# In a product-key expert layer, blocks of u are transposed in place, six buffers take gathered half rows, and their products stand four points behind the gathers

## The chip, the cores and the metric

One core of one Trainium2 chip. The metric is the time of one execution in device microseconds, the median of three runs: 3521.41 us (3520.7 to 3525.29). A difference of 0.2%, about 7 us, is what a measurement of this kernel can tell from none.

## The reference

One decoder layer over 512 tokens of width 2048, in float32. The first half is a modulated RMSNorm, one projection, a short causal convolution beside differential attention, and an output projection. The second half, in which the change lies, is a product-key expert layer: each token takes 16 of 16384 single-neuron experts in each of 8 heads.

```
h2 = RMSNorm(x) * (1 + scale2) + shift2
idx, g = top 16 of the 128 x 128 key sums, softmax of their scores     # per token and head
a = <u[idx], h2>                                                       # 128 dot products of width 2048 per token
w = gelu(a) * g
x = x + gate2 * sum(w * v[idx])                                        # u, v: 16384 x 2048 each
```

## The kernel before

**Two ways for the experts.** The first TG = 160 tokens are *gathered*: for each of 128 choices the rows of u and of v that the tokens chose are fetched by an indirect DMA and used on VectorE. The other TD = 352 tokens are *dense*: all 16384 experts are computed for them on TensorE, and a table of gates (`g_dram`) zeroes those not chosen. The gathered work fills VectorE, POOL and the DMA engines beside the dense matmuls.

**The dense path** goes over 128 blocks of 128 experts, in chunks of CH = 8. A block of u (1 MB) comes by eight DMAs of 128 KB (`u_load`, L511, on SP's queue) into a tile `ur`, of which there are two (UR_BUFS). Its layout needs the 32 x 32 blocks transposed: `u_turn` transposes one half at a time (L780, VectorE) into a tile `utf`, of which there are two; `split` then writes a float32r high part (L88, ScalarE) and the rest (L89, VectorE) into `ut`, of which there are two (UT_BUFS). TensorE takes 48 matmuls per block from it (L792), ScalarE the gelu (L809), `w_block` multiplies by the gates (L824) and splits into W. After eight blocks `v_group` loads v (`vr`, L935, 512 KB, three buffers), splits it into `vs` (L88, L89) and does as many matmuls again (L945); sums go to `acc` (L961). The first NPRE = 12 blocks are transposed earlier, beside the output projection (`u_ahead`, L516: `uar` into `uat`), and kept in `u_dram`.

**The gathered path.** There are 643 steps: for 128 choices of 128 tokens, and then for 32 rounds in which the last 32 tokens are folded four times into the partitions, each choice has two half rows of u, later two of v (`gathered`, L844, [128 x 1024], issued by POOL). A half row of u is multiplied by h2 and summed (L853), one of v is multiplied by its weight and added to `gacc` (L867, L869). All use tile `gt`, of which there are GBUF = 4. A gather also waits for the last matmul of a list `pace`, so that it doesn't run ahead of TensorE; a point is added to the list four times per block in u, and once per two blocks in `v_group`, and at each point `gather_to` emits the steps that are due, the product right behind its gather.

**What sets the order.** Each engine runs its queue in order. The order in the queues is set when the kernel is built, by a scheduler that takes the instructions' priorities from the program; a row of a queue waits for semaphores. SP's queue has the loads of u, v and the gates; its DMAs take eight semaphores in turn, so that each waits for the one eight before it to have landed.

**The end.** In the last chunk `add_gathered` brings the gathered tokens' sums (a_dram for the first 128, `gacc` for the folded 32) into the result `xs`, and `store` writes it out.

## Time and profile before

| | |
|---|---|
| median of the runs | 3521.41 us |
| the profiled execution | 3524.61 us, its span 3522.6 us |
| busy: TensorE / VectorE / ScalarE / POOL | 92% / 81% / 35% / 40% |
| mean granted TensorE clock | 0.967 |
| DMA | 896.34 MB, mean 254 GB/s |
| chain that ended last | DMA 42%, VectorE 28%, TensorE 15% |

The stretch from about 1500 to 3440 us is the main loop over the blocks; the weights of the first half come before it, the end of the last chunk after it. A line is that of the kernel before; `L89` and `L88` are the helper `split`, so that its uses are told apart by their tiles. VectorE's busy share is high but below that of TensorE, and what matters is what each idle stretch waited for.

### The profile page before, as it was taken

What the parts mean: (1) busy time and instruction counts of PE and PEld (TensorE: products, weight loads), DVE (VectorE), ACT (ScalarE), POOL (GpSimd) and SP (SyncE); (2) the same over time, 40 slices, a digit from 0 to 9 for tenths busy, and PEclk for the clock granted to TensorE, in tenths of its full rate; (3) what the DMA queues carried; (4) which work ended last, traced back from release to release, by engine and by line L of the source; (5) the groups of instructions that cost most, each with busy time, mean ns of one, the idle gap of its engine ahead of it and who ended that gap; (6) DMA issues with size and microseconds to landing.
All of it is one profiled execution on the core that took longest, in us unless ns stands there. A gap on an engine that the chain in (4) does not pass through costs nothing.

```text
span 3522.6 us, 49092 instructions
## 1 busy us (share of the span) xinstructions
...
## 2 busy tenths in 40 slices
...
GB/s 288 286 229 143 254 190 178 183 177 290 252 88 68 61 122 202 264 298 323 305 315 295 310 310 299 300 287 300 306 314 313 298 307 306 326 310 319 299 302 163
DMA packets 425712, 896.34 MB, mean 254 GB/s; under 512 B 40402, under 2 KB 119167, under 8 KB 420735
## 3 DMA queue, kind: packets, MB, share of 16 engines
...
HBM read 843.47 MB, written 49.55 MB: 254 GB/s over the span
## 4 chain that ended last, share of the span: by engine, by line
DMA 42%; DVE 28%; PE 15%; issue 9%; POOL 3%; SPq 2%; ACT 1%; DVEq 0%; POOLq 0%; ACTq 0%
DMA ur<-in_expert_u_dram 14%; DMA vr<-in_expert_v_dram 9%; DMA gt<-in_expert_u_dram,idxu 6%; PE pm L457 4%; DMA ada_w<-in_w_ada_dram 4%; DMA gt<-in_expert_v_dram,idxu 4%; DVE gacc L869 3%; DVE utf L780 3%; DVE vs L89 2%; DVE gt L907 2%; DVE gt L853 2%; DVE ut L89 2%; DVE ada_acc L196 2%; PE pm L547 2%; DVE run L196 2%
## 5 line engine op out<-in xcount | busy, mean ns | idle before, releaser
L792 PE MATMUL pa<-hd,ut 128*128 128x352 f32 x6144 | 1077.3, 328 | 63.9 <-DVE ut L89 41.0
L945 PE MATMUL pv<-W,vs 128*128 128x352 f32 x6144 | 1071.4, 328 | 50.6 <-DVE vs L89 27.0
L792 PEld LDWEIGHTS pa<-hd,ut 128*128 128x128 f32 x6144 | 1015.2, 191 | 75.8 <-DVE ut L89 48.4
L945 PEld LDWEIGHTS pv<-W,vs 128*128 128x128 f32 x6144 | 1014.5, 191 | 61.2 <-DVE vs L89 32.7
L89 POOL TENSOR_TENSOR wsp<-wraw,wsp 128x1024 fp32r<-128x1024 f32 x160 | 391.5, 2449 | 562.1 <-ACT wsp L88 530.3
L844 POOL DMA_INDIRECT gt<-in_expert_u_dram,idxu x256 | 343.9, 1344 | 626.4 <-DVE gt L853 309.8
L88 ACT ACTIVATE vs<-vr 128x1024 fp32r<-128x1024 f32 x256 | 271.3, 1060 | 819.2 <-DMA vr<-in_expert_v_dram 365.8
L844 POOL DMA_INDIRECT gt<-in_expert_v_dram,idxu x256 | 340.0, 1328 | 477.9 <-DVE gacc L869 341.5
L853 DVE SCALAR_TENSOR_TENSOR gt<-gt,h2n 128x1024 f32<-128x1024 f32 x320 | 386.2, 1215 | 104.9 <-DMA gt<-in_expert_u_dram,idxu 84.8
L869 DVE SCALAR_TENSOR_TENSOR gacc<-gt,ga_a,gacc 128x1024 f32<-128x1024 f32 x316 | 400.4, 1275 | 73.9 <-DMA gt<-in_expert_v_dram,idxu 48.5
L89 DVE TENSOR_TENSOR vs<-vr,vs 128x1024 fp32r<-128x1024 f32 x256 | 309.8, 1210 | 46.9 <-ACT vs L88 46.7
L88 ACT ACTIVATE ut<-utf 128x1024 fp32r<-128x1024 f32 x232 | 244.0, 1056 | 282.3 <-DVE utf L780 169.6
L780 DVE STREAM_TRANSPOSE utf<-ur 128x1024 f32<-128x1024 f32 x232 | 286.9, 1237 | 18.2 <-DMA ur<-in_expert_u_dram 14.1
L88 ACT ACTIVATE wsp<-wraw 128x1024 fp32r<-128x1024 f32 x160 | 169.1, 1058 | 368.1 <-issue 94.7
L89 DVE TENSOR_TENSOR ut<-utf,ut 128x1024 fp32r<-128x1024 f32 x232 | 281.9, 1215 | 9.6 <-ACT ut L88 9.5
L457 PE MATMUL pm<-big,wsp 128*128 128x512 f32 x1152 | 287.6, 402 | 0.0
L457 PEld LDWEIGHTS pm<-big,wsp 128*128 128x128 f32 x1152 | 215.2, 192 | 42.6 <-issue 0.2
L196 DVE SCALAR_TENSOR_TENSOR ada_acc<-ada_w,scol,ada_acc 128x512 f32<-128x512 f32 x195 | 208.3, 1068 | 28.5 <-DMA ada_w<-in_w_ada_dram 25.1
L245 PE MATMUL pqk<-wsp,big 128*128 128x512 f32 x768 | 193.3, 411 | 21.3 <-DVE qk L291 12.9
L701 PE MATMUL pm<-big,wsp 128*128 128x512 f32 x768 | 188.2, 402 | 16.1 <-POOL wsp L89 14.5
L245 PEld LDWEIGHTS pqk<-wsp,big 128*128 128x128 f32 x768 | 150.6, 199 | 57.6 <-DVE qk L291 15.9
L701 PEld LDWEIGHTS pm<-big,wsp 128*128 128x128 f32 x768 | 146.2, 193 | 48.5 <-POOL wsp L89 17.0
(274 smaller groups left out, 3195.4 us busy)
## 6 DMA issues: line engine op xcount, KB each, us to landing
vr<-in_expert_v_dram SPq DMA_DIRECT2D x256, 512.0 KB, 10.0
ur<-in_expert_u_dram SPq DMA_DIRECT2D x928, 128.0 KB, 9.2
...
g<-g_dram SPq DMA_DIRECT2D x32, 704.0 KB, 13.6
...
```

The costliest lines, as they stand in the source:

```text
L88: hi = nc.scalar.activation(dst[:, 0], src, AF.Copy)
L89: (eng or nc.vector).tensor_tensor(out=dst[:, 1], in0=src, in1=dst[:, 0].bitcast(F32), op=OP.subtract)
L196: nc.vector.scalar_tensor_tensor(new, wt[:, k], s, old, op0=OP.mult, op1=OP.add)
L245: nc.tensor.matmul(banks[i], hT[kk][:, a, i * P:(i + 1) * P], ws[:, b, k], start=(kk == last[0] and n == 0), stop=(kk == last[1] and n == 2))
L457: nc.tensor.matmul(banks[n2], ws[:, a, k, n2 * P:(n2 + 1) * P], hT[kk][:, b], start=(kk == 0 and n == 0), stop=(kk == KC - 1 and n == 2))
L701: nc.tensor.matmul(banks[j], ws[:, a, k, j * P:(j + 1) * P], h2T[kk][:, b], start=(kk == 0 and n == 0), stop=(kk == KC - 1 and n == 2))
L780: nc.vector.transpose(t, UR[0][:, :, q * 256:(q + 1) * 256].rearrange("p b (c r) -> p c b r", r=32))
L792: mm = nc.tensor.matmul(pa[:, :TD], ut[:, a, j], hd[k][:, b], start=(k == 0 and n == 0), stop=(k == KC - 1 and n == 2))
L844: d = nc.gpsimd.indirect_dma_start(out=t, out_offset=None, in_=src, in_offset=bass.IndirectOffsetOnAxis(ap=gidx[g][:, j:j + 1], axis=0), e ...
L853: nc.vector.scalar_tensor_tensor(t, t, 1.0, h2n[:, f * D // 2:(f + 1) * D // 2], op0=OP.mult, op1=OP.mult, accum_out=ga_a[:, f, j:j + 1])
L869: nc.vector.scalar_tensor_tensor(gacc[:, s], t, a, gacc[:, s], op0=OP.mult, op1=OP.add)
L945: mm = nc.tensor.matmul(pv[j // 2][:, j % 2, :TD], vs[:, a, bb, j * P:(j + 1) * P], W[e0 // 2][:, m, bb], start=(b == 0 and n == 0), stop= ...
```

## The change

- `u_turn` no longer has a tile `utf`: half a block is transposed in place inside `ur` (contiguous runs of 256), and `split` reads `ur` in the order that `utf` had. So `ur` is free for the next load only when both halves are split; before, when both were transposed.
- `u_ahead` transposes in place too; `uat` is gone, `uar` has three buffers; `u_dram` holds the other layout.
- The room of `utf` goes to two more `gt`: GBUF is 6.
- `gather_u` and `gather_v` give back the product as a function. `gather_to` holds it back until the list `pace` is LAG = 4 points longer, or six are held, or a step needs them all; it is then placed after the last point's matmul in the scheduler's order (no semaphore).
- The a_dram loads of `add_gathered` use the tiles `ot` of `store` (four of them).

```diff
-GBUF = 4
+GBUF = 6
+LAG = 4
-PU_BUFS = 1
+PU_BUFS = 3
-UTF_BUFS = 2
...
         def u_ahead(e):
-            ur = pu.tile([P, 4, 512], F32, name="uar")
+            ur = pu.tile([P, 4, 512], F32, name="uar", bufs=PU_BUFS)
             u_load(ur, e)
-            t = pu.tile([P, 4, 4, 4, 32], F32, name="uat", bufs=PU_BUFS)
-            for q in range(4):
-                u_quarter(t[:, q], ur, q)
-            nc.sync.dma_start(u_dram[e], t.rearrange("p q c b r -> p (q c b r)"))
+            for b in range(4):
+                nc.vector.transpose(ur[:, b], ur[:, b])
+            nc.sync.dma_start(u_dram[e], ur.rearrange("p b d -> p (b d)"))
...
-            if e < NPRE:
-                t = UR[0][:, 2 * q:2 * q + 2].rearrange("p a (c b r) -> p (a c) b r", c=4, b=4)
-            else:
-                t = up.tile([P, 8, 4, 32], F32, name="utf", bufs=UTF_BUFS)
-                nc.vector.transpose(t, UR[0][:, :, q * 256:(q + 1) * 256].rearrange("p b (c r) -> p c b r", r=32))
-            UT[n] = up.tile([P, 2, 8, P], F32R, name="ut", bufs=UT_BUFS)
-            split(UT[n], t.rearrange("p c b r -> p c (b r)"))
+            t = UR[0][:, :, q * 256:(q + 1) * 256]
+            if e >= NPRE:
+                nc.vector.transpose(t, t)
+            UT[n] = up.tile([P, 2, 8, 4, 32], F32R, name="ut", bufs=UT_BUFS)
+            split(UT[n], t.rearrange("p b (c r) -> p c b r", r=32))
...
         def gather_u(g, j, f):
             t = gathered(expert_u, g, j, f)
-            nc.vector.scalar_tensor_tensor(t, t, 1.0, h2n[:, f * D // 2:(f + 1) * D // 2], op0=OP.mult, op1=OP.mult,
-                                           accum_out=ga_a[:, f, j:j + 1])
+            return lambda: nc.vector.scalar_tensor_tensor(t, t, 1.0, h2n[:, f * D // 2:(f + 1) * D // 2],
+                                                          op0=OP.mult, op1=OP.mult, accum_out=ga_a[:, f, j:j + 1])
...
         done = [0]
+        held_back = []
+
+        def use_next():
+            i = held_back.pop(0)[1]()
+            if pace:
+                tc.add_manual_dep(i.ins, pace[-1].ins.name, ORDER, reason="rows have landed")
 
         def gather_to(blocks):
             first = 0.55 * CH
             frac = min(1.0, max(0.0, (blocks - first) / (NK - first - CH)))
+            while held_back and held_back[0][0] + LAG <= len(pace):
+                use_next()
             while done[0] < math.ceil(len(steps) * frac):
                 f, a = steps[done[0]]
-                f(*a)
+                while held_back and (len(held_back) == GBUF or f in (gather_w, gather_next)):
+                    use_next()
+                use = f(*a)
+                if use is not None:
+                    held_back.append((len(pace), use))
                 done[0] += 1
+            while held_back and frac == 1.0:
+                use_next()
...
-                ar = fin.tile([P, 512], F32, name="ar")
+                ar = fin.tile([P, T], F32, name="ot", bufs=4)
```

**VectorE's queue, a piece of the main loop.** Before: the first row transposes the second half of one block of u and so frees its `ur`; the second transposition begins the next block, the third ends it. `gacc<-gt` are products of gathered rows (they wait for a DMASW semaphore, the gather's landing, and for VectorE itself).

```order
L780 STREAM_TRANSPOSE utf<-ur 128x1024 [waits DVE_49]
L869 SCALAR_TENSOR_TENSOR gacc<-gt,ga_a,gacc 128x1024 [waits DMASW5_49,DVE_49]
L780 STREAM_TRANSPOSE utf<-ur 128x1024 [waits DMAHW4_49,DMAHW3_49,DMAHW5_49,DMAHW2_49,DMAHW6_49,DMAHW1_49,DMAHW7_49,DMAHW0_49,DVE_49]
L869 SCALAR_TENSOR_TENSOR gacc<-gt,ga_a,gacc 128x1024 [waits DMASW6_49,DVE_49]
L89 TENSOR_TENSOR ut<-utf,ut 128x1024 [waits PE_49,Activation_49]
L869 SCALAR_TENSOR_TENSOR gacc<-gt,ga_a,gacc 128x1024 [waits DMASW7_49,DVE_49]
L961 TENSOR_TENSOR acc<-acc,pv 128x704 [waits PE_49]
L869 SCALAR_TENSOR_TENSOR gacc<-gt,ga_a,gacc 128x1024 [waits DMASW0_49,DVE_49]
L961 TENSOR_TENSOR acc<-acc,pv 128x704 [waits PE_49]
L780 STREAM_TRANSPOSE utf<-ur 128x1024 [waits DVE_49]
```

Of the change, the same queue: the first row splits the second half of a block and frees its `ur`; the last is the first transposition of the block that is loaded into that very tile.

```order
L89 TENSOR_TENSOR ut<-ur,ut 128x1024 [waits PE_49,Activation_49]
L862 SCALAR_TENSOR_TENSOR gacc<-gt,ga_a,gacc 128x1024 [waits DMASW0_49,DVE_49]
L862 SCALAR_TENSOR_TENSOR gacc<-gt,ga_a,gacc 128x1024 [waits DMASW1_49,DVE_49]
L89 TENSOR_TENSOR vs<-vr,vs 128x1024 [waits Activation_49]
L89 TENSOR_TENSOR vs<-vr,vs 128x1024 [waits DMAHW3_49,Activation_49]
L862 SCALAR_TENSOR_TENSOR gacc<-gt,ga_a,gacc 128x1024 [waits DMASW2_49,DVE_49]
L862 SCALAR_TENSOR_TENSOR gacc<-gt,ga_a,gacc 128x1024 [waits DMASW3_49,DVE_49]
L89 TENSOR_TENSOR ut<-ur,ut 128x1024 [waits Activation_49]
L862 SCALAR_TENSOR_TENSOR gacc<-gt,ga_a,gacc 128x1024 [waits DMASW4_49,DVE_49]
L818 TENSOR_TENSOR ge<-ge,g_20447 128x704 [waits Activation_49]
L862 SCALAR_TENSOR_TENSOR gacc<-gt,ga_a,gacc 128x1024 [waits DMASW5_49,DVE_49]
L774 STREAM_TRANSPOSE ur<-ur 128x4x256 [waits DMAHW4_49,DMAHW5_49,DMAHW3_49,DMAHW6_49,DMAHW2_49,DMAHW7_49,DMAHW1_49,DMAHW0_49]
```

The row that frees `ur` was a transposition and is now the second split, which stands behind the next block's transpositions. Over 110 blocks of the main loop there are 12 to 39 rows from the row that frees a tile to the transposition of its next block before, 19.9 on average, and 9 to 19 now, 13.5 on average (9: 4 blocks, 10: 12, 11: 12, 12: 18, 13: 10, 14: 11, 15: 13, 16: 14, 17: 10, 18: 5, 19: 1). From the product that frees a `gt` to the product of its next gather there were 10 rows in the median, and are now 16. The queue has 13.6 rows per block in both.

**SP's queue in the main loop.** Before, three loads of v and one of u, of which the sixth row of u takes the semaphore of the first v:

```order
L935 DMA vr<-in_expert_v_dram 128x2x512 [waits DMAHW0_49,DVE_49]
L935 DMA vr<-in_expert_v_dram 128x2x512 [waits DMAHW1_49,DVE_49]
L935 DMA vr<-in_expert_v_dram 128x2x512 [waits DMAHW2_49,DVE_49]
L511 DMA ur<-in_expert_u_dram 32x2x512 [waits DMAHW3_49,DVE_49]
L511 DMA ur<-in_expert_u_dram 32x2x512 [waits DMAHW4_49]
L511 DMA ur<-in_expert_u_dram 32x2x512 [waits DMAHW5_49]
L511 DMA ur<-in_expert_u_dram 32x2x512 [waits DMAHW6_49]
L511 DMA ur<-in_expert_u_dram 32x2x512 [waits DMAHW7_49]
L511 DMA ur<-in_expert_u_dram 32x2x512 [waits DMAHW0_49]
```

Of the change:

```order
L942 DMA vr<-in_expert_v_dram 128x2x512 [waits DMAHW0_49,DVE_49]
L942 DMA vr<-in_expert_v_dram 128x2x512 [waits DMAHW1_49,DVE_49]
L511 DMA ur<-in_expert_u_dram 32x2x512 [waits DMAHW2_49,DVE_49]
L511 DMA ur<-in_expert_u_dram 32x2x512 [waits DMAHW3_49]
L511 DMA ur<-in_expert_u_dram 32x2x512 [waits DMAHW4_49]
L511 DMA ur<-in_expert_u_dram 32x2x512 [waits DMAHW5_49]
L511 DMA ur<-in_expert_u_dram 32x2x512 [waits DMAHW6_49]
L942 DMA vr<-in_expert_v_dram 128x2x512 [waits DMAHW7_49,DVE_49]
L511 DMA ur<-in_expert_u_dram 32x2x512 [waits DMAHW0_49]
```

The pattern stayed: 225 of the 928 loads of u take the semaphore of a load of v that stands up to eight rows ahead, and 31 that of the gates, in both kernels.

**VectorE's queue near the end.** Before, the last rows that update `xs` from `acc` are followed by fifteen products in a row, of which the first five stand here:

```order
L89 TENSOR_TENSOR vs<-vr,vs 128x1024 [waits DMAHW4_49,Activation_49]
L972 SCALAR_TENSOR_TENSOR xs<-acc,modc,xs 128x352 [waits DMAHW5_49]
L972 SCALAR_TENSOR_TENSOR xs<-acc,modc,xs 128x352 x3
L869 SCALAR_TENSOR_TENSOR gacc<-gt,ga_a,gacc 128x1024 [waits DMASW1_49,DVE_49]
L869 SCALAR_TENSOR_TENSOR gacc<-gt,ga_a,gacc 128x1024 [waits DMASW2_49,DVE_49]
L869 SCALAR_TENSOR_TENSOR gacc<-gt,ga_a,gacc 128x1024 [waits DMASW3_49,DVE_49]
L869 SCALAR_TENSOR_TENSOR gacc<-gt,ga_a,gacc 128x1024 [waits DMASW4_49,DVE_49]
L869 SCALAR_TENSOR_TENSOR gacc<-gt,ga_a,gacc 128x1024 [waits DMASW5_49,DVE_49]
```

Of the change, the last products:

```order
L862 SCALAR_TENSOR_TENSOR gacc<-gt,ga_a,gacc 128x1024 [waits DMASW3_49,DVE_49]
L862 SCALAR_TENSOR_TENSOR gacc<-gt,ga_a,gacc 128x1024 [waits DMASW4_49,DVE_49]
L89 TENSOR_TENSOR vs<-vr,vs 128x1024 [waits DMAHW3_49,Activation_49]
L862 SCALAR_TENSOR_TENSOR gacc<-gt,ga_a,gacc 128x1024 [waits DMASW5_49,DVE_49]
L862 SCALAR_TENSOR_TENSOR gacc<-gt,ga_a,gacc 128x1024 [waits DMASW6_49,DVE_49]
L89 TENSOR_TENSOR vs<-vr,vs 128x1024 [waits DMAHW4_49,Activation_49]
L862 SCALAR_TENSOR_TENSOR gacc<-gt,ga_a,gacc 128x1024 [waits DMASW7_49,DVE_49]
L979 SCALAR_TENSOR_TENSOR xs<-acc,modc,xs 128x352 [waits DMAHW6_49]
```

All products now stand ahead of the first update of `xs`, and ten splits of v come behind them; before, six did.

## Rows read from the trace of the kernel before

**Rows 1.** Busy time by stretches: start:end and length in us, then busy us (and instructions) of TensorE matmuls, weight loads, VectorE, ScalarE and POOL, the granted clock, the DMA share and GB/s.

```profile
1502.00:3378.00 1876.00, 1799.19 (x10943) 1781.94 (x10943) 1667.27 (x1821) 559.34 (x627) 805.67 (x599) 0.98 1.02 307
3000.00:3250.00 250.00, 245.26 (x1516) 243.57 (x1515) 228.01 (x261) 77.70 (x88) 115.05 (x82) 1.00 1.04 320
3380.00:3466.00 86.00, 38.65 (x190) 36.39 (x189) 62.94 (x72) 9.51 (x14) 39.81 (x29) 0.71 0.78 274
```

**Rows 2.** Groups of instructions in the stretch 1502 to 3378 us, costliest first: count, busy us, mean ns of one, then idle time of the engine just before them and what ended it.

```profile
L945 PE MATMUL pv<-W,vs 128*128 128x352 f32 x5574 | 963.9, 326 | 36.3 <-DVE vs L89 20.2 <-ACT vs L88 11.1 <-ACT W L88 3.0
L792 PE MATMUL pa<-hd,ut 128*128 128x352 f32 x5369 | 935.4, 326 | 40.5 <-DVE ut L89 20.8 <-ACT ut L88 19.5
L853 DVE SCALAR_TENSOR_TENSOR gt<-gt,h2n 128x1024 f32<-128x1024 f32 x311 | 375.3, 1215 | 98.7 <-DMA gt<-in_expert_u_dram,idxu 78.6 <-DMA gt<-in_expert_u_dram,ib 19.6
L869 DVE SCALAR_TENSOR_TENSOR gacc<-gt,ga_a,gacc 128x1024 f32<-128x1024 f32 x283 | 358.7, 1274 | 56.0 <-DMA gt<-in_expert_v_dram,idxu 48.5 <-DMA gt<-in_expert_v_dram,ib 6.7
L89 DVE TENSOR_TENSOR vs<-vr,vs 128x1024 fp32r<-128x1024 f32 x232 | 280.7, 1210 | 35.5 <-ACT vs L88 35.3
L780 DVE STREAM_TRANSPOSE utf<-ur 128x1024 f32<-128x1024 f32 x223 | 275.9, 1237 | 17.3 <-DMA ur<-in_expert_u_dram 13.3 <-DMA h2n<-h_dram 3.2 <-DMA vr<-in_expert_v_dram 0.8
L89 DVE TENSOR_TENSOR ut<-utf,ut 128x1024 fp32r<-128x1024 f32 x223 | 271.0, 1215 | 1.1 <-ACT ut L88 1.0
L89 DVE TENSOR_TENSOR W<-ge,W 128x704 fp32r<-128x704 f32 x57 | 50.2, 880 | 0.0
L824 DVE TENSOR_TENSOR ge<-ge,g 128x704 f32<-128x704 f32 x56 | 49.4, 883 | 0.0
```

**Rows 3.** Waits of POOL's gathers in 1500 to 3440 us (who waited for whom, us in total, times, longest), and the landing of a gather after its issue.

```profile
POOL gt L844 <- DVE gacc L869: 405.9, 197, 9.9
POOL gt L844 <- DVE gt L853: 400.3, 191, 5.3
POOL gt L844 <- PE pv L945: 77.7, 34, 4.8
POOL gt L844 <- PE pa L792: 32.3, 24, 3.8
...
DMA to landing us min/median/max: 4.2/9.2/13.2
```

**Rows 4.** Tile `ur` in 1500 to 3440 us: one DMA issue on SP's queue (ns, minimum, median, maximum), and the landing of one load of 128 KB after its issue.

```profile
L511 SPq DMA_DIRECT2D ur<-in_expert_u_dram x880: 311/419/3407, 1503.4 to 3351.9; - x176
...
DMA to landing us min/median/max: 3.4/9.3/18.0
```

**Rows 5.** Waits in SP's queue in 1440 to 3440 us: us in total, times, longest. L511 is u, L935 is v.

```profile
SPq L935 <- DVE vs L89: 407.9, 111, 10.6
SPq L511 <- DMA vr<-in_expert_v_dram: 309.0, 108, 5.4
SPq L511 <- DVE utf L780: 271.5, 91, 8.2
SPq L511 <- DMA ur<-in_expert_u_dram: 129.6, 165, 2.1
...
SPq L511 <- DMA g<-g_dram: 76.6, 24, 5.9
```

**Rows 6.** One load of u in the order of time (start, us, engine): the transposition that frees the tile, SP's eight issues, the transposition of the new block and its wait.

```profile
1863.76 1.24 DVE L780 STREAM_TRANSPOSE utf<-ur 128x1024 f32<-128x1024 f32 x1
1865.02 12.33 SPq L511 DMA_DIRECT2D ur<-in_expert_u_dram  x8
...
1879.33 1.23 DVE L780 STREAM_TRANSPOSE utf<-ur 128x1024 f32<-128x1024 f32 x1
1886.23 12.33 SPq L511 DMA_DIRECT2D ur<-in_expert_u_dram  x8
...
1906.07 1.25 DVE L780 STREAM_TRANSPOSE utf<-ur 128x1024 f32<-128x1024 f32 x1 [1.76 <-DMA ur<-in_expert_u_dram]
```

**Rows 7.** The chain that ended last, in order of time, near the end of the gathers: start, us, what.

```profile
3435.32 2.01 DVE gacc L869 x2
3437.64 2.48 DVE gacc L869 x2
3441.22 0.93 POOL gt L844
3442.46 5.75 DMA gt<-in_expert_v_dram,ib
3448.67 5.54 DMA gt<-in_expert_v_dram,ib
3454.30 2.59 DVE gacc L869 x2
3458.00 5.51 DMA gt<-in_expert_v_dram,ib
3463.59 1.29 DVE gacc L869
```

**Rows 8.** The transpositions ahead of the main loop, beside the output projection: ns minimum, median, maximum, first and last start.

```profile
L516 DVE STREAM_TRANSPOSE uat<-uar x48: 668/669/717, 811.7 to 934.6; 128x512 f32<-128x512 f32 x48
```

**Rows 9.** ScalarE's half of the split of u, over the whole execution: count, busy us, mean ns, idle before.

```profile
L88 ACT ACTIVATE ut<-utf 128x1024 fp32r<-128x1024 f32 x232 | 244.0, 1056 | 282.3 <-DVE utf L780 169.6
```

9 lines of the change are left out of this document (3 added, 6 removed).

## The prediction

> **What bounds the kernel now.** I read the stretches first. From 1502 to 3378 us, the main loop without its ends, TensorE is busy for 1799 of 1876 us, VectorE for 1667, and the DMA engines move 307 GB/s at a share of 1.02 [rows 1]. All three are near full, so the question is what ends the gaps. The groups of that stretch tell it [rows 2]: TensorE was idle for 36.3 + 40.5 = 77 us, and the releasers named are the splits of v and u on VectorE and ScalarE. VectorE was idle ahead of the products of gathered rows for 98.7 + 56.0 = 155 us, ahead of the splits of v for 35.5, ahead of the transpositions for 17.3; that is all but about 1 us of its 209 us of idle time. In its queue everything behind a product waits with it, the splits that TensorE needs too. So the waits of VectorE for gathers are the largest loss inside the loop.
>
> Why do they wait? A gather may be issued when the product four before it is done. POOL waited 405.9 + 400.3 us for such products and 77.7 + 32.3 for the pace of TensorE [rows 3]: the four buffers hold the gathers back, the pace hardly. In the median there are 10 rows of VectorE's queue between the product that frees a buffer and the one that uses it next. The loop has 223 transpositions, 111.5 blocks [rows 2], so a block takes 1876 / 111.5 = 16.83 us, of which 1667 / 111.5 = 14.95 are busy; with 13.6 rows per block a row is 1.10 us of work. Ten rows are 11 us, for an issue and a landing of 9.2 [rows 3]: no slack.
>
> **The change part by part.** *The gathers.* With six buffers and held products the distance is 16 rows in the median, 17.6 us, against the same 9.2 and an issue. I take the 155 us, 1.39 per block, as gone. From below: TensorE was idle for only 77 us, so if nothing else binds, no more than that comes out of the loop; that 16 rows are still too few is excluded by the 8 us to spare.
>
> *The loads of u.* Here the change takes away what it gave to the gathers. Before, a tile was free when both halves were transposed, and its next block's transposition stood 19.9 rows behind, 21.9 us of work and in truth more. Now the second split frees it, and the distance is 13.5 rows: 14.9 us of work. How long does a load take? Eight issues of 0.419 us are 3.4 us, the last lands 9.3 us later [rows 4]. Between the issues SP waits for the semaphore of an earlier DMA: 309.0 us for v, 76.6 for gates, 129.6 for earlier loads of u [rows 5]; over 116 loads 2.66, 0.66 and 1.12 us. The sum is 17.1 us. Two loads show it [rows 6]: in both SP needs 12.33 us for its eight issues, and in the second, freed at 1880.56 and begun at 1886.23, the transposition at 1906.07 had to wait. Before, such loads were covered; they cost 17.3 us in the whole loop [rows 2].
>
> After, the waits for earlier loads of u should be gone, since the earlier load has been transposed before the new one may start; those for v and gates stay, as SP's pattern does. That makes 16.0 us. Setting 16.0 against the 110 distances (9 to 19 rows of 1.10 us each) and counting only where the load is late gives 1.87 us per block; with 17.1 it is 2.61, and with 12.7 (no such wait at all) 0.35. These are the bounds. Landings scatter from 3.4 to 18.0 us [rows 4], and a late load adds while an early one gives nothing back, so I take **2.4 us per block**, nearer the upper end. It stands in VectorE's queue at the transposition, ten rows ahead of the split that TensorE needs: TensorE has a half block and some of v before it runs dry, but the delay comes every block, and VectorE has only 16.83 - 14.95 us of idle time to pay it from.
>
> The waits ahead of the splits of v, 35.5 us or 0.32 per block, I keep. So a block takes 14.95 + 0.32 + 2.4 = 17.67 us, 0.84 more than 16.83; over 111.5 blocks **+94 us**.
>
> *The end.* Before, fifteen products stand in a row behind the last updates of xs from acc, and the chain goes through them and through gathers that each wait for a product, from 3435.3 to 3464.9 us [rows 7]; TensorE is busy for 38.65 of the 86 us around it [rows 1]. After, all products stand ahead of the first update. I take these **-30 us**; the bounds are 0 (the rows of the update wait for their own loads just as long) and 86 - 38.65 = 47.
>
> *At nothing.* Transpositions in place: as many, of the same size, each over blocks of 32 x 32. The products of u already write their own input and take 1215 ns, as the split of u does that doesn't [rows 2]; a gain or loss of 22 ns (1237 against 1215) over 232 is 5 us. The splits read runs of 32 now: the product with the gates does too, and takes 883 ns where the split of W, with contiguous reads, takes 880. ScalarE, where no row shows such a read, is busy for 559 of 1876 us [rows 1]; without that cover a tenth more on 232 splits of 1056 ns [rows 9] would be 25 us. The 48 transpositions ahead of the loop, 669 ns each [rows 8], stay beside the output projection. The loads into ot instead of ar change which tile frees them, in the last 60 us; I put that at nothing, 5 us either way.
>
> **Sum:** 94 - 30 = +64 us. The profiled execution, 3524.6 us, is 3.2 above the median of the runs; the sum set on the median 3521.4 gives 3585 us.
>
> **Rivals.** *A, the gathers win* (the other side). Loads of v get issued well before those of u, because u now waits for its split and v doesn't; the semaphores that u needs are free by then, and a load takes 12.7 us. The loop then loses 0.35 us per block to u: 14.95 + 0.32 + 0.35 = 15.62, 1.21 below 16.83, 135 us in all. But TensorE had only 77 us of idle time, so -77 - 30 = -107: 3414 us. It decides at the load's time: at 15.4 us the loss is 1.5 us per block and the loop is even with before; with the 30 us of the end the kernel is even at about 15.9. My 16.0 is close to that, and this is why A is likely. For it speaks that in the second load of [rows 6] SP came late to u; against it that the semaphores of v are the largest wait (309.0 us) and SP's pattern is the same.
>
> *B, the DMA engines are the limit.* The share is 1.02 over the loop [rows 1], so more gathers in flight only land later, u is as late as now, and the loop stays as it is: -30 at the end, 3491 us, or nothing at all, 3521. Against it: from 3000 to 3250 us the engines moved 320 GB/s while TensorE was busy for 245 of 250 us; 307 / 320 of 1876 us would be 76 less, no tighter than TensorE.
> The Trainium skill, in DMA: Bandwidth & Descriptors, section Bandwidth, puts the limit from HBM for one core at about 358 GB/s; by that B would be out. No stretch here reaches it, and the share is at its top at 307, so the trace leaves B a chance that the page would not.
>
> *C, the change doesn't do what it says.* The products move, but gathers are issued no earlier (the pace holds them, or SP's loads push them back), and VectorE waits for both: with half of the 1.39 us left, 14.95 + 0.32 + 0.70 + 2.4 = 18.37 us per block, +172 - 30 = 3663 us. Against it stand the 806 us that POOL waited for buffers against 110 for the pace [rows 3].
>
> **How the numbers follow.** Forecast 0.52, with a range of its own from 3530 to 3640 us (1.9 to 2.9 us per block for u); A 0.28; B 0.14, of which half without the end's gain; C 0.06. What a measurement can tell from no change is 0.2%, 7 us. Within it lie half of B and a sliver of the forecast and of A around the even point: 0.08. Slower: 0.56; faster: 0.36. The range reaches from 3430, which takes in most of A, to 3665, beyond the forecast's own end and about where C lies, and leaves out 2 in 10.
>
> **What would show it.** Right, if VectorE's idle time ahead of the products falls below 40 us, and that ahead of the transpositions rises from 17 to some 270 us with u's load named; if POOL's waits for products shrink; if transpositions stay at 1237 ns and splits near 1215; if from about 3380 us TensorE no longer has a hole of 50 us. Wrong, if VectorE waits little for u (A), if a gather's landing goes well above 9.2 us at the same GB/s (B), or if the products still wait (C). If ScalarE's split of u takes well over 1056 ns, my price for the reads was wrong.

## The result and the profile after

3539.27 us (median of 11 runs, 3529.34 to 3550.69) against 3521.18 us of the kernel before on the same chip (11 runs): a ratio of 1.0061 [1.0042, 1.008]. The change makes the kernel slower by 0.6%, 18 us; the forecast was 64 us. The profiled execution took 3532.23 us, 7.6 more than that of before: it was 7 us quicker than its kernel's median, that of before 3 us slower than its own. So the two traces place 7.6 of the 18 us; the other 10 lie within the scatter of the runs.

The main loop got longer and the end shorter. The last split of u is a clean border, since each kernel has the same work behind it but for gathers that are late. The tile `ut` of before and of after (ns minimum, median, maximum; first and last start):

```profile
L89 DVE TENSOR_TENSOR ut<-utf,ut x232: 1178/1218/1293, 1435.8 to 3382.3; 128x1024 fp32r<-128x1024 f32 x116
```

```profile
core 0 of [0], span 3530.2 us
L89 DVE TENSOR_TENSOR ut<-ur,ut x256: 1169/1222/2439, 1199.9 to 3428.5; 128x1024 fp32r<-128x1024 f32 x128
```

The loop ends 3428.5 - 3382.3 = 46.2 us later, and what follows takes 3530.2 - 3428.5 = 101.7 us where it took 3522.6 - 3382.3 = 140.3, 38.6 less. The difference is the 7.6 us.

The stretches of after, columns as in [rows 1]: the loop, its slowest 500 us, and the end.

```profile
1502.00:3378.00 1876.00, 1763.84 (x10618) 1739.34 (x10617) 1633.71 (x1798) 543.52 (x611) 899.73 (x603) 0.97 0.98 305
2500.00:3000.00 500.00, 463.54 (x2780) 456.32 (x2779) 421.01 (x379) 141.51 (x158) 216.07 (x149) 0.97 0.95 287
3380.00:3466.00 86.00, 80.82 (x480) 79.25 (x479) 79.09 (x84) 24.05 (x31) 36.91 (x25) 0.96 0.86 286
```

In the loop the DMA share (the mean busy share of the 16 DMA engines; it can pass 1, so their records overlap) fell from 1.02 to 0.98, and between 2500 and 3000 us to 0.95 with 287 GB/s. At the end TensorE is busy for 80.82 of 86 us where it was for 38.65. The groups of 1502 to 3378 us that answer to [rows 2]:

```profile
L952 PE MATMUL pv<-W,vs 128*128 128x352 f32 x5381 | 941.4, 328 | 71.6 <-DVE vs L89 52.7 <-ACT vs L88 12.8 <-DVE W L89 3.1
L786 PE MATMUL pa<-hd,ut 128*128 128x352 f32 x5237 | 919.5, 327 | 40.5 <-ACT ut L88 21.3 <-DVE ut L89 18.6 <-issue 0.2
L847 DVE SCALAR_TENSOR_TENSOR gt<-gt,h2n 128x1024 f32<-128x1024 f32 x312 | 373.2, 1219 | 8.3 <-DMA gt<-in_expert_u_dram,idxu 6.9 <-DMA gt<-in_expert_u_dram,ib 1.3
L862 DVE SCALAR_TENSOR_TENSOR gacc<-gt,ga_a,gacc 128x1024 f32<-128x1024 f32 x285 | 360.0, 1278 | 0.0
L89 DVE TENSOR_TENSOR vs<-vr,vs 128x1024 fp32r<-128x1024 f32 x223 | 271.4, 1218 | 5.8 <-ACT vs L88 5.7
L89 DVE TENSOR_TENSOR ut<-ur,ut 128x1024 fp32r<-128x1024 f32 x218 | 265.9, 1221 | 1.1 <-issue 1.0
L774 DVE STREAM_TRANSPOSE ur<-ur 128x1024 f32<-128x1024 f32 x217 | 257.8, 1225 | 227.9 <-DMA ur<-in_expert_u_dram 126.2 <-DMA vr<-in_expert_v_dram 59.0 <-issue 42.7
```

Read the idle column. Ahead of the products 155 us became 8.3, ahead of the splits of v 35.5 became 5.8, ahead of the transpositions 17.3 became 227.9. VectorE's idle time did not shrink (242 us, 209 before): it moved to one place. There the releaser named is u's load for 126.2 of the 227.9 us, a load of v for 59.0, and nothing that the profile shows for 42.7. A transposition in place takes 1225 ns (1237), the split of u 1221 (1215).

SP's queue in 1440 to 3440 us (beside [rows 5]):

```profile
SPq L511 <- DVE ut L89: 301.6, 82, 9.5
SPq L511 <- DMA vr<-in_expert_v_dram: 174.9, 63, 5.5
SPq L511 <- DMA g<-g_dram: 77.9, 27, 6.0
SPq L511 <- DMA ur<-in_expert_u_dram: 69.0, 90, 1.8
```

u's waits for semaphores of v fell from 309.0 to 174.9 us, those for its own earlier loads from 129.6 to 69.0; in their place it waits for the split that frees its tile. POOL's waits for products fell from 806 ([rows 3]) to 633 us.

### The profile page after: what moved, and what is told of

Same layout as the page of the kernel before. It is cut to its first block, busy times and chain, and to the rows that moved or that the text cites. A ratio compares the mean times of both kernels' runs of the same rounds, so it can differ in the third digit from the quotient of the medians.

```text
span 3530.2 us, 49441 instructions
## 1 busy us (share of the span) xinstructions
PE 3239.9 (92%) x18006; PEld 2974.4 (84%) x18006; DVE 2830.2 (80%) x4261; ACT 1218.4 (35%) x1828; POOL 1511.8 (43%) x985
## 3 DMA queue, kind: packets, MB, share of 16 engines
q1 hardware_dynamic: 333310, 557.62, 51.6%
## 4 chain that ended last, share of the span: by engine, by line
DMA 34%; DVE 29%; PE 22%; issue 9%; SPq 3%; POOL 2%; ACT 1%; DVEq 0%; ACTq 0%; POOLq 0%
DMA ur<-in_expert_u_dram 16%; DMA vr<-in_expert_v_dram 6%; PE pm L457 5%; DMA ada_w<-in_w_ada_dram 4%; PE pv L952 4%; PE pm L543 4%; DMA g<-g_dram 4%; PE pa L786 3%; DVE gt L847 3%; DVE ut L89 3%; DVE ur L774 2%; DVE ada_acc L196 2%; DVE vs L89 2%; DVE gacc L862 2%; SPq L511 2%
## 5 line engine op out<-in xcount | busy, mean ns | idle before, releaser
L838 POOL DMA_INDIRECT gt<-in_expert_u_dram,idxu x256 | 379.1, 1481 | 554.0 <-PE pv L952 285.1
L838 POOL DMA_INDIRECT gt<-in_expert_v_dram,idxu x256 | 376.8, 1472 | 478.9 <-DVE gacc L862 319.0
L774 DVE STREAM_TRANSPOSE ur<-ur 128x1024 f32<-128x1024 f32 x232 | 275.6, 1225 | 231.4 <-DMA ur<-in_expert_u_dram 128.7
L88 ACT ACTIVATE ut<-ur 128x1024 fp32r<-128x1024 f32 x256 | 269.8, 1055 | 414.5 <-PE pa L786 125.6
L89 DVE TENSOR_TENSOR ut<-ur,ut 128x1024 fp32r<-128x1024 f32 x256 | 314.5, 1230 | 15.4 <-ACT ut L88 14.3
L457 PE MATMUL pm<-big,wsp 128*128 128x512 f32 x1152 | 286.1, 400 | 0.0
L457 PEld LDWEIGHTS pm<-big,wsp 128*128 128x128 f32 x1152 | 214.0, 191 | 42.2
L697 PE MATMUL pm<-big,wsp 128*128 128x512 f32 x768 | 186.3, 400 | 12.3 <-POOL wsp L89 10.8
L543 PE MATMUL pm<-big,wsp 128*128 128x512 f32 x768 | 182.4, 397 | 5.0 <-DVE x L549 2.6
```

The source lines that it names most:

```text
L88: hi = nc.scalar.activation(dst[:, 0], src, AF.Copy)
L89: (eng or nc.vector).tensor_tensor(out=dst[:, 1], in0=src, in1=dst[:, 0].bitcast(F32), op=OP.subtract)
L457: nc.tensor.matmul(banks[n2], ws[:, a, k, n2 * P:(n2 + 1) * P], hT[kk][:, b], start=(kk == 0 and n == 0), stop=(kk == KC - 1 and n == 2))
L543: nc.tensor.matmul(banks[j], ws[:, a, k, j * P:(j + 1) * P], yT[kk0 + k][:, b], start=(kq == 0 and k == 0 and n == 0), stop=(kq == 7 and k ...
L774: nc.vector.transpose(t, t)
L838: d = nc.gpsimd.indirect_dma_start(out=t, out_offset=None, in_=src, in_offset=bass.IndirectOffsetOnAxis(ap=gidx[g][:, j:j + 1], axis=0), e ...
```

## The experiments

"Queue theory" is the forecast's reasoning: the distance in VectorE's queue from the row that frees a buffer to the row that uses its next content, against a landing of given length, decides what waits. "DMA theory" is rival B grown up: the DMA engines move some 305 GB/s of this mixture, every landing is as long as that makes it, and distances only say who waits. The runs were made in several sessions on different chips, each beside the kernel before; so runs of different sessions are compared by their ratios. Idle times of VectorE, GB/s and share in the table are of 1502 to 3378 us; of e12, e16 and e18, whose loops ended at 3315 to 3324 us, a little of the end is in them. Where a loop moves the same bytes, its GB/s are its time said once more; the share is the figure that tells whether the engines had gaps.

| | ratio to before [95%] | idle ahead of transpositions / products / splits of v | GB/s, share |
|---|---|---|---|
| before | 1 | 17 / 155 / 36 | 307, 1.02 |
| after | 1.0061 [1.0042, 1.008] | 228 / 8 / 6 | 305, 0.98 |
| e1 in place alone | 1.0344 [1.0322, 1.0366] | 165 / 153 / 0 | 288, 0.94 |
| e2 six, no LAG | 1.0107 [1.0085, 1.0129] | 218 / 31 / 3 | 303, 0.99 |
| e3 LAG, four buffers | 1.0312 [1.0282, 1.0342] | 132 / 163 / 2 | 291, 0.96 |
| e4 third ur, four buffers | 1.0289 [1.0266, 1.0312] | 134 / 156 / 2 | 292, 0.94 |
| e5 turned late | 1.0177 [1.0151, 1.0203] | 107 / 40 / 71 | 304, 0.99 |
| e6 four loads of u | 1.0162 [1.0122, 1.0202] | 229 / 20 / 9 | 302, 0.98 |
| e7 = e5 and e6 | 1.0271 [1.0236, 1.0307] | 120 / 65 / 71 | 299, 0.99 |
| e8 before, four loads | 1.0120 [1.0095, 1.0145] | 10 / 195 / 31 | 302, 1.01 |
| e9 half tiles, mid | 1.0046 [1.0017, 1.0076] | 87 / 28 / 110 | 302, 1.02 |
| e10 turned mid | 1.0120 [1.0081, 1.0159] | 155 / 35 / 48 | 303, 0.99 |
| e11 = e10, half of u | 0.9847 [0.9815, 0.9878] | 33 / 35 / 63 | 285, 0.89 |
| e12 before, half of u | 0.9712 [0.9682, 0.9742] | 0 / 97 / 21 | 289, 0.90 |
| e13 = e10, half of v | 1.0041 [1.0016, 1.0066] | 85 / 50 / 60 | 277, 0.93 |
| e14 before, 5 gt, 2 vr | 1.0025 [0.9998, 1.0051] | 41 / 27 / 141 | 305, 1.00 |
| e15 before, 5 gt, 1 utf | 1.0397 [1.0343, 1.045] | 37 / 257 / 7 | 290, 0.95 |
| e16 = e14, two passes | 1.0039 [1.0015, 1.0064] | 29 / 22 / 162 | 301, 1.00 |
| e17 u unread | 0.9957 [0.9936, 0.9978] | 0 / 34 / 137 | 311, 1.02 |
| e18 = e17, two passes | 0.9886 [0.9855, 0.9917] | 0 / 13 / 166 | 307, 1.01 |

### The parts of the change: e1, e2, e3

e1 is the transposition in place with four buffers and each product right behind its gather, so both of these edits of the changed kernel; e2 has the second alone (six buffers, no held products), e3 the first alone (four buffers, products held back).

```diff
-GBUF = 6
+GBUF = 4
...
-                    held_back.append((len(pace), use))
+                    use()
```

> In place alone: the changed kernel with four buffers for gathered rows and each product emitted right behind its gather, as before. In its queue the transposition of a block stands 11.5 rows (12.7 us of work) behind the split that frees its tile, against 13.5 in the changed kernel. Theory (load time against queue distance): 16 us of load against these distances is 3.3 us of waiting per block where the same sum gave 1.9 for the changed kernel and 2.1 was measured, so about 3.5 us per block, 390 us of idle time ahead of the transpositions; the gathers' waits (155 us before) shrink, since the gathers land while VectorE waits for u; total 3700 to 3780 us. Rival (contention: the loads of u are late because six gathers share the DMA engines with them): with four gathers the wait for u is nearly gone, under 60 us, the gathers' waits are back, and the total is 3500 to 3545 us.

> In place and six buffers, but each product emitted right behind its gather (no LAG). The distances in the queue are as in the changed kernel: 13.5 rows for u, 16 for a gather. Theory: it is the distance that counts, and the number of buffers sets it, so the same time within 0.4%, 3525 to 3555 us, idle ahead of products under 30 us, ahead of transpositions 190 to 260 us. Rival (holding the products back is what took the gathers' waits away): idle ahead of products is back above 100 us, and the total is 3580 us or more, or the waits change places and the total is the same.

> In place and LAG = 4, but four buffers for gathered rows. Distances: 11.4 rows for u, 10 for a gather. Theory: LAG without buffers does nothing, so this is as e1: idle ahead of transpositions about 390 us, total 3700 to 3780 us, within 0.5% of e1. Rival (LAG alone does it): idle ahead of products falls well below that of e1, and the total is at least 1% below e1.

Columns as above, of e1:

```profile
1502.00:3378.00 1876.00, 1724.51 (x10248) 1695.66 (x10247) 1559.48 (x1716) 522.98 (x586) 769.59 (x563) 0.96 0.94 288
L847 DVE SCALAR_TENSOR_TENSOR gt<-gt,h2n 128x1024 f32<-128x1024 f32 x305 | 367.8, 1216 | 93.5 <-DMA gt<-in_expert_u_dram,idxu 69.5 <-DMA gt<-in_expert_u_dram,ib 18.8 <-issue 3.9
L862 DVE SCALAR_TENSOR_TENSOR gacc<-gt,ga_a,gacc 128x1024 f32<-128x1024 f32 x254 | 322.5, 1277 | 59.1 <-DMA gt<-in_expert_v_dram,idxu 58.5 <-DVE gacc L862 0.4
L774 DVE STREAM_TRANSPOSE ur<-ur 128x1024 f32<-128x1024 f32 x208 | 246.6, 1222 | 164.9 <-DMA ur<-in_expert_u_dram 107.2 <-DMA vr<-in_expert_v_dram 42.7 <-issue 14.8
```

In place alone costs 3.4%. With four buffers the wait for u (165 us) comes on top of that for gathers (153, as before), and the DMA engines run partly empty (0.94). Two more buffers give 84 us of it back (e1 to e2), LAG another 16 by the ratios with six buffers (e2 to after) and 9 with four (e1 to e3), which the intervals don't tell from nothing. The gain at the end is the buffers' work, not LAG's: from the last split of u to the end e1 takes 131.6 us, e3 151.3, e2 93.3, after 101.7.

The queue theory had the order of the three, e3 within 0.5% of e1 among it, and not the size. For e1 and e3 it asked for some 390 us ahead of the transpositions and 3700 us or more; 165 and 132 us came, 3649 and 3640 us in all. The under 60 us of e1's rival didn't come either. e2 took 3565 us, 10 above its range.

### Where the transposition stands: e4, e5, e10, e9

e4 is e3 with a third tile. e5 and e10 are the changed kernel with an order in VectorE's queue: behind the last (e5) or the middle (e10, j == 3, shown here) matmul of the half that last read the ut tile.

```diff
+                if n - 2 in LAST:
+                    tc.add_manual_dep(tr.ins, LAST[n - 2].ins.name, ORDER, reason="turned late")
...
+                    if j == 3:
+                        LAST[e * 2 + q] = mm
```

> The changed kernel with the room spent otherwise: three buffers for blocks of u, four for gathered rows. The scheduler used the third buffer to turn blocks earlier still, 25 rows ahead of their split; from the split that frees a tile to the transposition that needs its next block there are again 11.4 rows. Theory (the transposition's place in the queue decides, not the number of buffers): VectorE waits for u as in e1, 300 to 420 us, total 3680 to 3780 us. Rival (two buffers are too few): the third buffer covers the load, idle ahead of transpositions under 60 us, the gathers' waits are back, total 3490 to 3530 us.

> The changed kernel, and a transposition is placed in the scheduler's order behind the last matmul that reads the ut tile which its split will take. In VectorE's queue it then stands 5 rows ahead of its split instead of 10 to 15, and 16.5 rows behind the split that freed its tile instead of 13.5. Theory (the place in the queue decides): 16 us of load against these distances is 1.07 us per block where it was 1.87, so the idle time ahead of transpositions falls from 228 to some 110 to 140 us per 1876 us, a block takes about 16.4 us, and the total is 3420 to 3480 us, faster than before. Rival (the DMA engines are the limit): the waits only change their place, total 3520 to 3550 us. A second rival (the early place covered ScalarE and VectorE between load and matmul): TensorE waits for ut more, total 3550 us or more.

> The changed kernel with the second of those edits alone: a transposition ordered behind the middle matmul of the half that last read its ut tile; whole tiles of u as in the changed kernel. 15.1 rows from the split that frees a tile to its next transposition (13.5 without the order, 16.5 with the later one of e5). Queue theory: idle ahead of the transpositions between 228 and 107 us, about 160; the waits that the later order brought (70 us ahead of the splits of v, 107 us of TensorE ahead of u's matmuls) at most half as large; 3535 to 3565 us. DMA theory: the sum of the waits is as in e5, 3570 to 3590 us.

e4 cured nothing (134 us, e3 132): the scheduler put the transposition as much earlier as the tile came free earlier, 11.4 rows again. That is neither the theory's 300 us and more nor the rival's cure. e5 has 16.5 rows and halves the wait for u, as the queue theory asks, and is slower than after, as its second rival had it:

```profile
L788 PE MATMUL pa<-hd,ut 128*128 128x352 f32 x5114 | 925.3, 334 | 106.9 <-DVE ut L89 66.9 <-ACT ut L88 40.0
L89 DVE TENSOR_TENSOR vs<-vr,vs 128x1024 fp32r<-128x1024 f32 x219 | 265.5, 1212 | 70.5 <-ACT vs L88 70.3
L774 DVE STREAM_TRANSPOSE ur<-ur 128x1024 f32<-128x1024 f32 x212 | 262.1, 1238 | 106.6 <-DMA ur<-in_expert_u_dram 66.0 <-issue 25.4 <-DMA vr<-in_expert_v_dram 9.8
```

The waits went to the splits of v (70.5 us) and to TensorE ahead of u's matmuls (106.9, after 40.5), which now get their splits late. e10 lies between (155 us). Its 3571 us are 6 above the queue theory's range and just inside the DMA theory's; the waits that the order brings were not halved, 48 us ahead of the splits of v (70.5 in e5) and 76 of TensorE ahead of u's matmuls (106.9).

e9 has e10's order and gives each half of u its own tile, freed by its own split; 20.8 rows.

```diff
-                UR[0] = up.tile([P, 4, 512], F32, name="ur", bufs=UR_BUFS)
+            t = up.tile([P, 4, 256], F32, name="ur", bufs=2 * UR_BUFS)
...
+                nc.sync.dma_start(t[s * 32:(s + 1) * 32],
+                                  expert_u[e * P:(e + 1) * P, c:c + 256].rearrange("(b r) d -> r b d", r=32))
```

> The changed kernel with two edits: a half of a block of u has a tile of its own (four of 512 KB, as much room as two of 1 MB), loaded by four DMAs of 128 KB in runs of 1 KB and freed by its own split; and a transposition is ordered behind the middle matmul (j = 3) of the half that last read the ut tile it will be split into. From the split that frees a half tile to the transposition of its next half there are 20.8 rows of VectorE's queue (13.5 in the changed kernel, 19.9 before); the gathers keep 16. Queue theory: the idle time ahead of the transpositions falls from 228 us to under 60, that ahead of the products stays under 30, so VectorE loses at most half of what it lost before (209 us in 1502 to 3378 us); TensorE, busy for 1799 / 111.5 = 16.14 us per block, binds: up to 77 us less than the kernel before in the loop and 42 less at the end, 3405 us at best; I say 3450, since the first late order of turns moved waits to the splits of v and to TensorE. DMA theory: landings grow, the engines move no more than 308 GB/s, and waits come back elsewhere: 3480 to 3520 us.

No gain to be seen against after, and 90 us above what I said. The wait for u fell to 87 us, not under 60; the splits of v took 110; the share is 1.02 with 302 GB/s. Here the DMA theory named what came, but its time was too low as well, by 23 us.

### The loads themselves: e6, e8, e7

e6 loads u with four DMAs of 256 KB in place of eight of 128 KB; e8 does that to the kernel before; e7 is e5 and e6 together.

```diff
-            for b in (0, 2):
-                for s in range(4):
-                    nc.sync.dma_start(t[s * 32:(s + 1) * 32, b:b + 2],
-                                      expert_u[e * P + b * 32:e * P + b * 32 + 64, s * 512:(s + 1) * 512]
-                                      .rearrange("(b r) d -> r b d", r=32))
+            for s in range(4):
+                nc.sync.dma_start(t[s * 32:(s + 1) * 32],
+                                  expert_u[e * P:(e + 1) * P, s * 512:(s + 1) * 512]
+                                  .rearrange("(b r) d -> r b d", r=32))
```

> The changed kernel with a block of u loaded by four DMAs of 256 KB instead of eight of 128 KB. That saves four issues of 0.42 us and half of the waits for a semaphore eight DMAs back, so a load should take some 13 to 14 us instead of 16 to 17. The scheduler moves the transposition up as well, to 11.6 rows (12.8 us) behind the split that frees the tile. Theory (load time against distance): about 1.0 to 1.5 us per block are left, total 3440 to 3500 us. Rival (DMA limit): the load takes as long as before, and with the shorter distance the total is 3600 us or more.

> The kernel before with a block of u loaded by four DMAs. Its transposition has 20 rows, and u cost it only 17 us of waiting. Theory: the gathers' waits stay, so 3500 to 3525 us; fewer issues may give v's loads a little. Rival (SP's queue and its eight semaphores bound both kernels): 3470 us or less.

> Both: transpositions placed late and u loaded by four DMAs. Distance 16.3 rows (17.9 us) against a load of 13 to 14 us. Theory: idle ahead of transpositions under 70 us, ahead of products under 20; VectorE's 15 us of work and TensorE's 15.4 us per block remain, total 3400 to 3460 us. Rival (DMA limit): no faster than e5 and e6, and the landing of a load grows as the loop gets shorter; total 3480 to 3550 us.

The waits of u's rows for earlier loads all but vanished (in e6 15.6 us for u's own, none for v; in e8 9.4), and both kernels became slower: 1.2% in e8, 1.0 in e6 against after; e7 loses 2.1% against after, about what e5 and e6 lose together. None of the three lies in a range that was named.

In e8 u's distance stayed (20 rows). There the landings grew, u's from 9.3 to 11.0 us (at twice the bytes a piece), v's from 10.0 to 11.5, the gathers' from 9.2 to 9.5, and the products wait for 195 us: what SP no longer waits for is waited for at the landing.

e6 doesn't show that. There the load did get shorter: counted in the records, blocks whose transposition had to wait took 17.1 us from the split that freed the tile in after, and 14.7 in e6. But the transposition also moved up, from 13.5 to 11.6 rows, and the idle time stayed at 229 us. So SP's waits, of which the ones for v stand in the prediction's sum with 2.66 us per block, were part of a load's time, as forecast.

### Fewer bytes: e11, e12, e13

Only the first four of u's eight DMAs per block, with bs = (0,) from block 14 on (e12 in the kernel before, e11 in e10), or the first block of each pair of v (e13 in e10). Tiles that stay allocated keep the rest of the data, so all other work is the same.

```diff
-        def u_load(t, e):
-            for b in (0, 2):
+        def u_load(t, e, bs=(0, 2)):
+            for b in bs:
...
+                nv = 2 if ch == 0 and dg == 0 else 1
+                ld = nc.sync.dma_start(vr[:, 0:nv], expert_v[e0 * P:(e0 + nv) * P, dg * 512:(dg + 1) * 512]
```

> The kernel before with only the first four of the eight DMAs of each block of u from block 14 on (half of u left out there). Its window for u (19.8 rows) and that for gathers (10) are as before. Queue theory: u was hardly late before (17 us in the loop), the gathers wait because ten rows are as long as their issue and landing; landings stay near 9.2 us, the 155 us ahead of the products stay above 100 and the time falls by at most 40 us. DMA theory: the gathers land sooner (under 8 us), their waits fall under 80 us, and the time falls by 50 to 80 us to where TensorE binds.

> e10 with only the first four of the eight DMAs of each block of u from block 14 on (half of u is left out there; the tile keeps what it held, so all other work is the same). The window is 14.4 rows. Queue theory: a load is four issues of 0.42 us, the waits for semaphores and a landing of some 9 us, about 12.7 us against 15.8 of work in the window: the idle time ahead of the transpositions falls under 60 us, the landing of one DMA stays near 9 us and the time falls by 50 to 110 us against e10. DMA theory: with 57 MB less of some 575 in the loop every landing gets shorter (under 7.5 us for u, under 8 for gathers) and the share of the DMA engines stays near 1 while the loop gets shorter by a tenth, until TensorE binds.

> e10 (the changed kernel, turned midway) with only the first block of each pair of blocks of v loaded, after the first four loads (half of v is left out there; the tile keeps what it held). u's eight loads per block and its window (15.0 rows, 15.1 in e10) are as in e10. Queue theory: a load of u takes as long as before but for shorter waits for the semaphores of v; the 155 us ahead of the transpositions stay above 100, and the time within 40 us of e10's 3571. DMA theory: with as many bytes taken away as in e11, all landings shorten as they did there (u from 8.4 to about 6.9, gathers from 9.3 to about 7.3), the wait for u falls under 60 us, and the time is e11's: 3475, within 25.

e12 takes 105 us off a kernel that waited 17 us for u. Its loop, one group and the landing of a gathered half row (9.2 us before, [rows 3]):

```profile
1502.00:3300.00 1798.00, 1764.42 (x10807) 1750.54 (x10806) 1666.84 (x1820) 556.20 (x622) 824.74 (x611) 0.99 0.91 290
...
L855 DVE SCALAR_TENSOR_TENSOR gt<-gt,h2n 128x1024 f32<-128x1024 f32 x309 | 372.2, 1215 | 77.4 <-DMA gt<-in_expert_u_dram,idxu 63.5 <-DMA gt<-in_expert_u_dram,ib 13.1
...
DMA to landing us min/median/max: 4.2/7.0/14.3
```

The share is 0.91, gathers land in 7.0 us and loads of u in 6.4 (9.3); the queue theory allowed a gain of 40 us. The DMA theory is right on the landings, and its gain of 50 to 80 us was too small; the products still waited for 97 us, not under 80. It is the bytes that count here, not the number of loads: e8 has as few loads of u, and its rows of u wait as little in SP's queue for earlier DMAs, with all the bytes, and it is slower than before.

e11 gains 98 us on e10, within what the queue theory allows; the landings are the DMA theory's (of u 6.9, of gathers 7.3, where the queue theory had 9), but its share near 1 didn't come (0.89): TensorE, busy for 499 of the 500 us from 2500, binds. e13 takes as many bytes away and gains only 31, as the queue theory had it, though the wait for u fell below its 100 us:

```profile
1502.00:3378.00 1876.00, 1757.32 (x10584) 1737.21 (x10584) 1660.21 (x1814) 548.87 (x608) 849.20 (x618) 0.97 0.93 277
...
L774 DVE STREAM_TRANSPOSE ur<-ur 128x1024 f32<-128x1024 f32 x217 | 268.9, 1239 | 85.2 <-DMA ur<-in_expert_u_dram 62.4 <-issue 13.9 <-DMA h2n<-h_dram 5.1
```

At a share of 0.93 the engines have gaps, and u, whose load is whole, is still late. So distances matter too, and the DMA theory alone doesn't do. The trace of e13 gives no landings, and its order is not quite e10's (its shortest windows of u are 6 rows, e10's 10), so the two effects are not separated to the last here.

### Nobody waits for u, and TensorE has less to do: e17, e18, e16

In e17 the blocks of u from 13 on are loaded by the same DMAs, each block begun at the same split, into a tile that nobody reads; transpositions and splits take block 12 again and again. With that one tile the scheduler's order is not quite that of after: from a block's second split to the transposition two blocks on there are 11.7 rows in the records (13.5).

```diff
+                    if after is not None:
+                        tc.add_manual_dep(d.ins, after.ins.name, SYNC, reason="as if its tile had been read")
...
+                elif e == NPRE:
+                    u_load(UR[0], e)
                 else:
-                    u_load(UR[0], e)
+                    u_load(URS[1], e, FREE.pop(e - 2))
```

e18 is e17, and e16 is e14 (below), with `enumerate(PASSES[:2])` in the matmuls of u and v.

> The changed kernel with the blocks of u from 13 on loaded as they are now, by as many DMAs and each begun when the second split of the block two before is done, but into a tile that nobody reads; the transpositions and splits take a tile that stays (block 12, turned again and again), so that the data of u are left out and the wait for them too; all other work and all bytes stay. The gathers' distance is 16 rows. Queue theory: VectorE loses the 2.10 us per block ahead of the transpositions and little comes in their place: 15.06 + 0.1 per block, so TensorE's 16.1 to 16.3 bind, 315 to 320 GB/s in the loop: about 3430 us. DMA theory: the loop stays above 16.6 us per block, the engines move no more than 310 GB/s, and waits ahead of the splits of v and the products take u's place: 3465 to 3510 us.

> e17 with only the first two of the three products in the matmuls of u and v (the third is left out): TensorE has a third less to do, so it can't bind. Queue theory: 15.1 to 15.5 us per block, 335 GB/s or more: 3290 to 3340 us. DMA theory: 16.6 us per block or more, at most 310 GB/s and a share of 1.0: 3450 to 3500 us, as e17 or little less.

> e14 with only the first two of the three products in the matmuls of u and v (the third is left out), so TensorE has a third less to do in the loop, about 10.8 us per block; VectorE's 14.95 and the bytes are the same. Windows: u 23.0 rows, gathers 14, v 12.7. Queue theory: landings stay at 9 to 10 us, all windows but v's are longer than that, and the loop runs at VectorE's pace, 15.2 to 15.6 us per block and 330 to 340 GB/s: 3300 to 3360 us. DMA theory: no more than 320 GB/s, 16.1 us per block or more, a share of 1.0 or more, landings above 9 us: 3430 to 3480 us.

e17, loop, and groups of 1502 to 3378 us:

```profile
1502.00:3300.00 1798.00, 1709.87 (x10409) 1697.64 (x10408) 1606.00 (x1774) 531.04 (x597) 811.78 (x591) 0.98 1.02 310
...
L858 DVE SCALAR_TENSOR_TENSOR gt<-gt,h2n 128x1024 f32<-128x1024 f32 x315 | 375.9, 1211 | 33.4 <-DMA gt<-in_expert_u_dram,idxu 27.1 <-DMA gt<-in_expert_u_dram,ib 6.0
L89 DVE TENSOR_TENSOR vs<-vr,vs 128x1024 fp32r<-128x1024 f32 x232 | 281.6, 1214 | 136.7 <-ACT vs L88 136.3
L781 DVE STREAM_TRANSPOSE ur<-ur 128x1024 f32<-128x1024 f32 x221 | 273.1, 1236 | 0.1
```

e18, and then e16, loop and a stretch behind it:

```profile
1502.00:3300.00 1798.00, 1338.13 (x7256) 1288.42 (x7254) 1598.43 (x1754) 553.04 (x623) 750.74 (x557) 0.88 1.02 307
3400.00:3450.00 50.00, 0.69 (x2) 0.29 (x2) 43.03 (x35) 0.39 (x2) 35.44 (x31) 0.50 0.94 344
```

```profile
1502.00:3300.00 1798.00, 1348.39 (x7238) 1302.82 (x7237) 1581.80 (x1725) 545.19 (x621) 730.69 (x542) 0.87 1.01 301
3400.00:3450.00 50.00, 0.00 (x0) 0.00 (x0) 38.47 (x31) 0.00 (x0) 37.19 (x31) 0.50 0.91 322
```

228 us of waiting taken away are worth 37 us by the ratios, 1.0% (29 by the medians, 3510.07 against 3539.27): 137 come back ahead of the splits of v, 34 ahead of the products. The share is 1.02 again. The queue theory had 3430 us; the DMA theory's range ends at 3510, so e17 stands at its very edge, and with 311 GB/s a little above its 310. With TensorE idle for a quarter of the loop (460 of 1798 us) the engines still move 307 GB/s in e18, and 301 in e16, which is as long as before. The queue theory wanted 330 and more in both, and its times are some 150 us and more too low; the DMA theory has e18 (3487 us) and is 55 us too low for e16 (3535). Dense blocks do get done sooner there (the last split of u stands at 3323.5 and 3321.2), but the gathers are then behind and run alone to 3450 us and later. That part of the result no theory had: the 3430 to 3480 us for e16 left the late gathers out.

### Another buffer without taking from u: e14, e15

The kernel before with a fifth `gt`, its room taken from `vr` (e14) or `utf` (e15, `UTF_BUFS` 2 to 1 and `VR_BUFS` left at 3).

```diff
-GBUF = 4
+GBUF = 5
-VR_BUFS = 3
+VR_BUFS = 2
```

> The kernel before with GBUF 5 and VR_BUFS 2 (products right behind their gathers, utf as before): the window of u stays (20.4 rows, 19.9 before), that of the gathers is 13 rows (10 before), that of v 13.3 (19.9 before). Queue theory: the waits ahead of the products fall from 155 us under 50, those for u stay small, v's 13.3 rows (14.6 us) are enough for a landing of 10; TensorE binds: -77 in the loop and -40 at the end, about 3410 us. DMA theory: the loop stays at 16.7 to 16.9 us per block and 305 to 310 GB/s, the waits move to the splits of v and the transpositions, and only the end gains: 3480 to 3500 us, I say 3490.

> The kernel before with GBUF 5 and UTF_BUFS 1: the window of u is 21.2 rows, that of the gathers 12; a transposition now stands 5 rows ahead of its split (9.7 before). Queue theory: -77 in the loop less some waits of TensorE for late splits, -40 at the end: 3420 to 3460 us. DMA theory: loop as before, end 40 less, and waits of TensorE for late splits as in e5: 3480 to 3520 us.

e14's groups of 1502 to 3378 us:

```profile
L853 DVE SCALAR_TENSOR_TENSOR gt<-gt,h2n 128x1024 f32<-128x1024 f32 x310 | 371.7, 1212 | 27.0 <-DMA gt<-in_expert_u_dram,idxu 21.2 <-DMA gt<-in_expert_u_dram,ib 5.5
L89 DVE TENSOR_TENSOR vs<-vr,vs 128x1024 fp32r<-128x1024 f32 x229 | 278.3, 1215 | 140.8 <-ACT vs L88 136.1 <-issue 4.4
```

e14 is as fast as before: the products' waits fell from 155 to 27 us, those ahead of the splits of v rose from 36 to 141, at 305 GB/s and a share of 1.00. The waits changed places, as the DMA theory had it. Its end is 29 us shorter, but its loop, which was to stay, is 34 longer, so the 3490 us were 45 too low. e15 went against both: the products wait for 257 us and TensorE for 150 ahead of u's matmuls. That a transposition which must wait for the one `utf` delays TensorE, and TensorE's pace the gathers (POOL waited 455 us for v's matmuls, 78 before), fits the trace but was not tried. No version tried computes everything and beats the kernel before.

## Why the prediction was wrong

The side was right; the size was 64 us for 18. The side hangs on a difference of 8 us in the traces, between a loop that is 46 us longer (94 forecast) and an end that is 39 shorter (30 forecast), so it is luck in part.

By its steps, per block: 217 transpositions are 108.5 blocks, so a block takes 1876 / 108.5 = 17.29 us after, where it took 16.83.

- *The gathers' 155 us are gone*: right (8.3; under 40 was asked).
- *In place costs nothing*: right. 1225 ns against 1237 for a transposition, 1221 against 1215 for VectorE's split, 1055 against 1056 for ScalarE's, which now reads runs of 32.
- *u's wait, 2.4 us per block*: the place and the cause are as forecast; measured 227.9 / 108.5 = 2.10, with u's load named for more than half. From the split that frees a tile to the next transposition there were 17.0 us on average in the records, and 17.1 in the blocks that had to wait (16.0 forecast for a load). But the sum behind it doesn't carry over: for e1 it gave 3.3 us per block, and 164.9 / 104 = 1.59 came. It turned rows into time by their work alone, 1.10 us a row. In e1, blocks whose load was not late had 14.6 us for some 11.4 rows: waits elsewhere in the queue give a load time.
- *The waits ahead of the splits of v, 0.32, I keep*: wrong. They fell to 0.05.
- *Busy time 14.95*: 15.06, since 5.5 products stand in a block's time where 5.3 did; the wait ahead of the products that is left is 0.08. So 15.06 + 2.10 + 0.05 + 0.08 = 17.29. Against the forecast 17.67 u accounts for -0.30, v for -0.27, the other two for +0.19.
- *The end, -30*: 38.6 by the last split of u.

The step that failed is the sum: "So a block takes 14.95 + 0.32 + 2.4 = 17.67 us". It adds a new wait to one that is taken to stay, and the two were not independent: v's 0.32 became 0.05, and u's 2.4 was 2.10. The 0.38 us between 17.67 and 17.29 are 42 us over 111.5 blocks, most of the 48 by which the loop was forecast too long.

Why do waits not add? e17 shows the exchange backwards: take the wait for u away, and 137 us appear ahead of v. e14 shows it in the kernel before: take the products' wait away, and the splits of v wait. In before the DMA share was 1.02, and whichever transfer stood with the shortest distance was waited for. A reading that fits all the runs, though none shows each step of it: a wait for u lets the other transfers catch up, until the engines have gaps; only then does it cost. e1 fits as the other half: with four buffers the engines had gaps (0.94), and there the wait for u came on top of the products' 153 us.

So of the 46 us that the loop lost, e17 gives back 31 (its last split of u is at 3397.3). For the other 15 the gathers that come sooner are enough: from 1502 to 3378 us the gathers' queue moved 313.67 MB before, 316.45 after and 322.01 in e17, and the 8.3 MB that e17 has more are an estimated 27 us at its 311 GB/s. What comes sooner isn't left for the end.

Of the rivals, B named the limit, and I set it at 0.14 because 250 us at 320 GB/s looked like slack (that row's share is 1.04, above the 1.02 that the prediction calls the top). Over the whole loop no kernel here that moves all the bytes moved more than 311 GB/s. But a share of 1 is no fixed rate. For 50 us the kernel after moved more, with TensorE never idle:

```profile
1550.00:1600.00 50.00, 50.00 (x313) 50.00 (x313) 45.94 (x61) 15.46 (x18) 29.60 (x20) 1.00 1.04 360
```

By the Trainium skill (DMA: Bandwidth & Descriptors, section Bandwidth), with its some 358 GB/s of HBM as one core's limit, B would have been out; the trace reaches that for these 50 us and disagrees for the loops: 307 at a share of 1.02 in e18, with TensorE idle for a quarter of the time. B's own outcome, 3491, didn't come either: the share fell to 0.98. Its sign, a longer landing, can't be read, as the view of after gives no landings. A rested on TensorE's 77 us as the floor; with u never late e17 takes 3510, not 3414.

The same section's rule to batch transfers to 1 MiB would have u in larger DMAs. No run here loads 1 MiB at once; the step towards it, 256 KB for 128, made e8 slower by 1.2%.

Open: what sets the 299 to 311 GB/s of the loops with a share of 0.99 and more, the engines, the memory behind them or the pace at which SP lets its loads go (in e17 and e18 u's rows still wait for loads of v for 316 and 372 us; e8 took such waits from the kernel before and gained nothing); and what e15's slowness rests on.
